# Softmax over 16384 rows: four of eight loads, and their stores, as four transfers of every fourth partition

## The chip, the core and the metric

The kernel runs on one core of one Trainium2 chip. The metric is the device time of one execution in microseconds (us); lower is better. Times given are medians of several runs. An execution under the profiler gives the trace and its page; the page's span runs from the first to the last recorded instruction.

## The reference

```
def setup_inputs():
    batch, seq, dim = 16, 1024, 512
    return {"x": np.random.randn(batch, seq, dim).astype(np.float32)}

def reference(x):
    x_max = np.max(x, axis=-1, keepdims=True)
    exp_x = np.exp(x - x_max)
    return (exp_x / np.sum(exp_x, axis=-1, keepdims=True)).astype(np.float32)
```

It is a softmax over the last dimension: 16384 rows of 512 fp32 values, 33.55 MB read and 33.55 MB written.

## The kernel before

The 16384 rows are cut into 16 groups of 1024 rows; a group (2 MB) is 8 rows on each of the 128 partitions. Two groups make one load and one store of 4 MB, so there are eight loads, L0 to L7, and eight stores, S0 to S7; store k writes the rows that load k brought. In a load, partition p gets 16 neighbouring rows of x, which is one run of 32 KB in the memory, and the 128 partitions together one run of 4 MB (`in_dram`, where x is viewed as `"(p r) d -> p r d"`). A store is the same in the other direction.

In SBUF the groups lie in a ring of 12 places (`RING`), six loads. So L0 to L5 need no wait, and L6 and L7 take the places of L0 and L1 and have to wait until S0 and S1 have landed (`before`, `stored`).

All transfers are issued by SP, on one queue. The first six loads are issued at the head of the program, the very first one even ahead of the opening barrier (`AT_HEAD`, `loads_at_the_head`). A closing barrier of the head (`tc.close()`, line 179) follows the six; the other engines begin their work after it. After that SP goes through a list written by hand:

```
ORDER = """
S0 S1 L6 L7 S2 S3 S4 S5 S6 S7
"""
```

Before a store SP waits until both groups of it are scaled (`store_scaled`), before L6 and L7 until the store of the old rows has landed. At the end it waits for the stores that are still out (line 200). The queue works in the order of issue.

The compute on a group g has three steps. VectorE (DVE) takes the negated maximum of each row (`rowmax`, line 145; one instruction for one or two groups), once the load has landed. ScalarE (ACT) computes the exponential in place with the maximum as bias and the row sum as a second output (`exp`, line 134; 8 rows for each partition and group, one instruction for each, in a loop `exps` over the groups). Then DVE takes the reciprocal of the sums (line 159), and DVE or GpSimd (POOL) multiplies the group by it (line 161, `scale`). DVE's order is written out too:

```
SEQUENCE = """
M0 M1 M2 D0 M3 D1 MM4 P2 MM6 D3 P4 MM8 D5 P6 MM10 D7 P8 MM12 D9 P10 MM14 D11 P12 D13 D14
D15
"""
```

M and MM are maxima of one and two groups, D a scaling on DVE and P one on POOL. Each load has a semaphore of its own, `loaded`; the DMA engines add 16 to it when a transfer has landed.

Of the kernel before, what the change touches and what calls it, by code (L numbers as in the profile page):

```python
# [15 lines left out]
GROUP = 8  # L16
# [4 lines left out]
STORES = [2, 2, 2, 2, 2, 2, 2, 2]  # L21
GROUPS = sum(LOADS)
LOAD_AT = [sum(LOADS[:k]) for k in range(len(LOADS))]
STORE_AT = [sum(STORES[:k]) for k in range(len(STORES))]

ORDER = """
S0 S1 L6 L7 S2 S3 S4 S5 S6 S7
# [32 lines left out]
@with_exitstack  # L60
def kernel(
    ctx: ExitStack,
    tc: tile.TileContext,
    x: bass.AP,
    out: bass.AP,
):
    nc = tc.nc
    nc.at_finalize(loads_at_the_head)
    P = nc.NUM_PARTITIONS

    x_rows, out_rows = x.flatten_outer_dims(), out.flatten_outer_dims()
    d = x_rows.shape[1]
    assert x_rows.shape[0] == P * GROUPS * GROUP

    def sbuf(name, n):
        return ctx.enter_context(nc.sbuf_tensor(name, [P, n], F32))

    ring = sbuf("ring", RING * GROUP * d)

    stat = sbuf("stat", RING * GROUP)  # L80
    recip = sbuf("recip", RING * GROUP)

    def sem(name):
        return ctx.enter_context(nc.semaphore(name))

    maxima, summed, inverted = [sem(s) for s in ("maxima", "summed", "inverted")]
    loaded = [sem(f"loaded{k}") for k in range(len(LOADS))]
    scaled = [sem(f"scaled{k}") for k in range(len(STORES))]

    def load_of(g):  # L90
        return max(k for k in range(len(LOADS)) if LOAD_AT[k] <= g)

    def store_of(g):
        return max(k for k in range(len(STORES)) if STORE_AT[k] <= g)


    before = {
        k: store_of(LOAD_AT[k] + LOADS[k] - 1 - RING)
        for k in range(len(LOADS))
        if LOAD_AT[k] >= RING  # L100
    }

    awaited = sorted(set(before.values()))
    stored = {k: sem(f"stored{k}") for k in awaited}
    others = sem("others")

    def at(g):
        return g % RING

    def rows(g, groups=1):  # L110
        part = ring[:, at(g) * GROUP * d : (at(g) + groups) * GROUP * d]
        return part.rearrange("p (r d) -> p r d", d=d)

    def cols(t, g, groups=1):
        return t[:, at(g) * GROUP : (at(g) + groups) * GROUP]

    def in_dram(t, g, groups):
        k = load_of(g)
        assert load_of(g + groups - 1) == k
        part = t[P * GROUP * LOAD_AT[k] : P * GROUP * (LOAD_AT[k] + LOADS[k]), :]  # L120
        first = (g - LOAD_AT[k]) * GROUP
        part = part.rearrange("(p r) d -> p r d", p=P)
        return part[:, first : first + groups * GROUP, :]

    def load(k):
        g, n = LOAD_AT[k], LOADS[k]
        return nc.sync.dma_start(out=rows(g, n), in_=in_dram(x_rows, g, n))

    def store(k):
        g, n = STORE_AT[k], STORES[k]  # L130
        return nc.sync.dma_start(out=in_dram(out_rows, g, n), in_=rows(g, n))

    def exp(row, one):
        return nc.scalar.activation(  # L134
            out=row, in_=row, func=EXP, bias=one, scale=1.0, accum_out=one
        )

    def spread(t):
        return t.unsqueeze(2).to_broadcast([P, GROUP, d])


    def rowmax(g, groups):
        assert load_of(g) == load_of(g + groups - 1)
        nc.vector.wait_ge(loaded[load_of(g)], 16)  # L144
        nc.vector.reduce_max(  # L145
            out=cols(stat, g, groups), in_=rows(g, groups), axis=AX, negate=True
        ).then_inc(maxima, groups)

    def exps():
        with nc.Fori(0, GROUPS, 1, engines=(ACT,)) as g:  # L150
            nc.scalar.wait_ge(maxima, 1).then_inc(maxima, -1)  # L151
            row = nc.scalar.snap((g % RING) * GROUP)
            for r in range(GROUP):
                done = exp(ring[:, bass.ds((row + r) * d, d)], stat[:, bass.ds(row + r, 1)])
            done.then_inc(summed, 1)

    def scale(g, engine):
        nc.vector.wait_ge(summed, g + 1)
        nc.vector.reciprocal(out=cols(recip, g), in_=cols(stat, g)).then_inc(inverted, 1)  # L159
        engine.wait_ge(inverted, g + 1)  # L160
        engine.tensor_mul(  # L161
            out=rows(g), in0=rows(g), in1=spread(cols(recip, g))
        ).then_inc(scaled[store_of(g)], 1)

    def done_by(k):
        later = [a for a in awaited if a >= k]
        return stored[later[0]] if later else others

    def store_scaled(k):
        nc.sync.wait_ge(scaled[k], STORES[k])  # L170
        store(k).then_inc(done_by(k), 16)


    with tc.manual_schedule(engines={SP}):
        for k in range(min(before)):
            first = load(k).then_inc(loaded[k], 16)
            tc.info.no_tile_sem_insts.add(first.ins.name)
    tc.close()
    tc.compile()  # L179

    nc.scalar.preload_act_table(EXP)  # L181
    exps()
    for work in SEQUENCE.split():
        kind = work.rstrip("0123456789")
        g = int(work[len(kind) :])
        if kind in ("M", "MM"):
            rowmax(g, len(kind))
        else:
            scale(g, nc.vector if kind == "D" else nc.gpsimd)
    for transfer in ORDER.split():  # L190
        k = int(transfer[1:])
        if transfer[0] == "S":
            store_scaled(k)
        else:
            last = before[k]
            since = max([a for a in awaited if a < last], default=-1)
            nc.sync.wait_ge(stored[last], 16 * (last - since))
            load(k).then_inc(loaded[k], 16)
    nc.sync.wait_ge(others, 16 * (len(STORES) - 1 - max(awaited)))
    nc.sync.nop()  # L200


# [28 lines left out]
```

## Time and profile before

| | before |
|---|---|
| median of 3 runs | 160.0 us (159.95 to 160.03) |
| the profiled execution's own time | 160.08 us |
| its span | 158.8 us |
| DVE busy | 121.8 us (77%) |
| ACT busy | 92.2 us (58%) |
| POOL busy | 42.3 us (27%) |
| DMA queue | 67.11 MB in 2304 packets, 98.9% of 16 engines' span, 423 GB/s in the mean |

On the page the DMA line gives the mean busy share of the core's 16 DMA engines in tenths, in 40 slices of the span (9 is 90% or more). A packet is what one DMA engine moves in one piece: here a run of 32 KB, or a completion of 4 bytes, which adds to the semaphore. In the rows by stage the columns are: the stretch in us and its length, the busy time of DVE, ACT and POOL in it with the number of instructions, the clock of TensorE (which has no work here), the DMA engines' share and the GB/s they moved. "SPq" is the issuing of a transfer by SP; the transfer itself takes place later, on the DMA engines.

### The profile page before, as it was taken

The page shows a single profiled execution, that of the slowest core. Times are in us where ns is not written, and L with a number is a line of the kernel's source. Part 1 is how long each engine was busy: PE and PEld are TensorE (multiplying, and loading weights), DVE is VectorE, ACT ScalarE, POOL GpSimd, SP SyncE. Part 2 cuts the span into 40 slices and gives each one's busy share as a digit, 9 for nine tenths or more (in the row PEclk, how much of TensorE's full clock was granted, in tenths as well). Part 3 has the DMA queues.
Part 4 walks back from the last instruction along what each step waited for, and adds up shares of the span by engine and source line. Part 5 has one row for each costly group of instructions (what it writes and reads, how often), then busy time and mean ns, then how long its engine had stood idle before and what let it go on. Part 6 is the DMA issues. An engine that isn't in the chain of part 4 may idle for free.

```text
span 158.8 us, 572 instructions
## 1 busy us (share of the span) xinstructions
DVE 121.8 (77%) x36; ACT 92.2 (58%) x257; POOL 42.3 (27%) x10
## 2 busy tenths in 40 slices
DVE  0008979999999999999999499999999999700000
ACT  0300699969406999999988990899599300000000
POOL 0000000000007903930970790079049300000000
DMA  7999999999999999999999999999999999999996
GB/s 264 438 479 405 405 495 421 396 438 471 413 405 438 471 405 396 396 413 471 438 396 462 446 413 405 454 421 438 438 421 446 413 446 438 438 421 438 429 429 264
DMA packets 2304, 67.11 MB, mean 423 GB/s; under 512 B 256, under 2 KB 256, under 8 KB 256
## 3 DMA queue, kind: packets, MB, share of 16 engines
q1 hardware_dynamic: 2304, 67.11, 98.9%
HBM read 33.55 MB, written 33.55 MB: 423 GB/s over the span
## 4 chain that ended last, share of the span: by engine, by line
DMA 45%; DVE 39%; issue 2%; DVEq 0%
DMA ring<-in_x_dram 26%; DVE ring L161 22%; DMA out_dram<-ring 20%; DVE stat L145 16%; DVE recip L159 1%; DVEq L144 0%
## 5 line engine op out<-in xcount | busy, mean ns | idle before, releaser
L134 ACT ACTIVATE ring<-ring,stat x128 | 90.4, 707 | 28.1 <-ACTq L151 28.1
L145 DVE TENSOR_REDUCE stat<-ring 128x16 f32<-128x8192 f32 (+1 forms) x10 | 69.5, 6956 | 15.7 <-DMA ring<-in_x_dram 15.7
L161 POOL TENSOR_TENSOR ring<-ring,recip 128x4096 f32<-128x4096 f32 x6 | 42.1, 7016 | 81.8 <-DVE recip L159 81.8
L161 DVE TENSOR_TENSOR ring<-ring,recip 128x4096 f32<-128x4096 f32 x10 | 51.1, 5109 | 0.3
L134 ACT ACTIVATION_READ_ACCUMULATOR ring<-ring,stat x128 | 23.8, 186 | 0.0
L181 ACT ACT_TABLE_LOAD x1 | 1.3, 1283 | 4.0 <-PEq L179 4.0
L159 DVE RECIPROCAL recip<-stat 128x8 f32<-128x8 f32 x16 | 3.0, 190 | 0.0
L215 POOL MEMSET const-float32-0.0<- 128x1 f32 x1 | 0.1, 98 | 0.2 <-issue 0.2
L215 POOL MEMSET const-bfloat16-1.0<- 128x1 bf16 x1 | 0.1, 102 | 0.0
L215 POOL MEMSET const-uint8-127<- 128x1 uint8 x1 | 0.1, 102 | 0.0
L215 POOL MEMSET const-float32-1.0<- 128x1 f32 x1 | 0.1, 98 | 0.0
## 6 DMA issues: line engine op xcount, KB each, us to landing
ring<-in_x_dram SPq DMA_DIRECT2D x8, 4096.0 KB, 25.9
out_dram<-ring SPq DMA_DIRECT2D x8, 4096.0 KB, 24.0
```

The costliest lines, as they stand in the source:

```text
L134: return nc.scalar.activation(out=row, in_=row, func=EXP, bias=one, scale=1.0, accum_out=one)
L145: nc.vector.reduce_max(out=cols(stat, g, groups), in_=rows(g, groups), axis=AX, negate=True).then_inc(maxima, groups)
L159: nc.vector.reciprocal(out=cols(recip, g), in_=cols(stat, g)).then_inc(inverted, 1)
L161: engine.tensor_mul(out=rows(g), in0=rows(g), in1=spread(cols(recip, g))).then_inc(scaled[store_of(g)], 1)
L181: nc.scalar.preload_act_table(EXP)
L215: nc = _bacc.Bacc("TRN2", target_bir_lowering=False, num_devices=1)
```

## The change

A list `PIECES` gives for each load the number of transfers that it is made of: four for loads 0, 2, 5 and 7, one for the others. Where it is four, the load's 4 MB in the memory are cut into four pieces of 1 MB, each one run. Piece j goes to the partitions j, j + 4, j + 8 and so on, 32 of them, 16 rows (32 KB) to each. So other partitions than before hold the rows. The store of the same rows uses the same pieces. All are issued by SP, one after the other, where the one transfer was issued. They add to the same semaphore as the one transfer did, and the waits are for four times 16. The first load's first piece alone stands ahead of the opening barrier, since `AT_HEAD` still says one. The instructions of DVE, ACT and POOL are the same.

```
+PIECES = [4, 1, 4, 1, 1, 4, 1, 4]
...
-        part = part.rearrange("(p r) d -> p r d", p=P)
-        return part[:, first : first + groups * GROUP, :]
-
-    def load(k):
+        n = PIECES[k]
+        part = part.rearrange("(n q r) d -> n q r d", n=n, q=P // n)
+        return [part[j, :, first : first + groups * GROUP, :] for j in range(n)]
+
+
+    def load(k, done):
         g, n = LOAD_AT[k], LOADS[k]
-        return nc.sync.dma_start(out=rows(g, n), in_=in_dram(x_rows, g, n))
-
-    def store(k):
+        ones = [
+            nc.sync.dma_start(out=rows(g, n)[j :: PIECES[k]], in_=part).then_inc(done, 16)
+            for j, part in enumerate(in_dram(x_rows, g, n))
+        ]
+        return ones
+
+    def store(k, done):
         g, n = STORE_AT[k], STORES[k]
-        return nc.sync.dma_start(out=in_dram(out_rows, g, n), in_=rows(g, n))
+        by = PIECES[load_of(g)]
+        for j, part in enumerate(in_dram(out_rows, g, n)):
+            nc.sync.dma_start(out=part, in_=rows(g, n)[j::by]).then_inc(done, 16)
+
+    def store_count(first, last):
+        return 16 * sum(PIECES[load_of(STORE_AT[k])] for k in range(first, last))
...
-        nc.vector.wait_ge(loaded[load_of(g)], 16)
+        nc.vector.wait_ge(loaded[load_of(g)], 16 * PIECES[load_of(g)])
...
-        store(k).then_inc(done_by(k), 16)
+        store(k, done_by(k))
...
-            first = load(k).then_inc(loaded[k], 16)
-            tc.info.no_tile_sem_insts.add(first.ins.name)
+            for one in load(k, loaded[k]):
+                tc.info.no_tile_sem_insts.add(one.ins.name)
...
-            nc.sync.wait_ge(stored[last], 16 * (last - since))
-            load(k).then_inc(loaded[k], 16)
-    nc.sync.wait_ge(others, 16 * (len(STORES) - 1 - max(awaited)))
+            nc.sync.wait_ge(stored[last], store_count(since + 1, last + 1))
+            load(k, loaded[k])
+    nc.sync.wait_ge(others, store_count(max(awaited) + 1, len(STORES)))
```

## The prediction

> **What bounds the kernel now.** I read the page first, from its busy shares and its queue to its chain, then the rate stage by stage, then the joints between transfers in the trace's packet records.
>
> ```profile
> span 158.8 us, 572 instructions
> DVE 121.8 (77%) x36; ACT 92.2 (58%) x257; POOL 42.3 (27%) x10
> ...
> DMA  7999999999999999999999999999999999999996
> ...
> DMA packets 2304, 67.11 MB, mean 423 GB/s; under 512 B 256, under 2 KB 256, under 8 KB 256
> q1 hardware_dynamic: 2304, 67.11, 98.9%
> ```
>
> No compute engine is full, but the sixteen DMA engines are busy in every slice. Of the 2304 packets 256 are completions (16 transfers on 16 engines); the other 2048 are rows of 32 KB, 128 for each engine. 98.9% of 158.8 us over 128 rows is 1.227 us a row, and in the packet records 1.213 us is the usual one. 128 x 1.213 = 155.3 us, so only some 3.5 us of the span are anything but rows at their steady rate.
>
> The page's chain crosses DVE lines (39%), which could mislead: it follows the semaphores back, and the last store waits there for nothing but the queue. S7 is issued at 137.84, right after the last DVE multiply, while S6, issued at 128.69, ends near 148.1; S7's rows move from 148.1 to 158.27. So compute has 10 us in hand at the end. Earlier, L6 is issued at 71.08, when S1's rows are still moving until 79.8, and S2 at 81.46, when L6 and L7 have the queue until 99.6. The queue never runs dry, and the time is that of the DMA stream alone.
>
> The rates by stage show where the 3.5 us lie (the stages are cut where transfers begin; the last column is GB/s):
>
> ```profile
> 0.00:11.60 11.60, 0.00 (x0) 1.28 (x1) 0.20 (x4) 1.00 0.93 376
> 11.60:50.40 38.80, 37.03 (x11) 24.33 (x69) 1.68 (x1) 1.00 1.01 435
> 50.40:60.70 10.30, 10.27 (x3) 10.30 (x29) 5.34 (x1) 1.00 1.00 404
> 60.70:89.80 29.10, 27.57 (x10) 27.94 (x81) 15.41 (x3) 1.00 1.00 434
> 89.80:99.60 9.80, 8.87 (x3) 5.60 (x16) 5.64 (x1) 1.00 1.01 428
> 99.60:158.80 59.20, 38.07 (x12) 22.80 (x64) 14.03 (x2) 1.00 0.97 421
> ```
>
> 435 GB/s is the steady rate. L0 runs at 376: 11.6 x (1 - 376/435) = 1.57 us lost, 1.04 of it before the first packet, 0.53 in the slow first rows. L5, the load ahead of the first store, runs at 404: 10.3 x (1 - 404/435) = 0.73 us. L7, the load ahead of S2, runs at 428: 0.16 us. The rest is the tail: the engines' last rows end between 157.06 and 158.27, and the last landing is at 158.73. The packet records agree: L5's last row on each engine takes 1.79 us in the mean instead of 1.213, L7's 1.36, L0's first 1.92; at the other joints, loads after loads, stores after stores and L6 after S1, the rows keep their pace within 0.01 us in the mean. On the engine that I follow to the latest end, 158.27, these stretches are 0.62 (start), 0.96 (L5 to S0) and 0.41 us (L7 to S2).
>
> The profiled execution took 160.08 us, 1.28 more than its span; the median is 160.0. I make the sum against 160.08 and take the 0.08 off at the end.
>
> **The change part by part.** *Bytes and rows*: nothing is removed. Every row still has 32 KB in both memories, so there are still 2048 rows, 128 x 1.213 us for each engine if each transfer of 32 rows is spread over all sixteen, two rows each. No instruction of DVE, ACT or POOL changes in size or number.
>
> *Completions*: loads 0, 2, 5, 7 and stores 0, 2, 5, 7 are four transfers each: 24 more, so 24 more completions on every engine. A completion takes 9 ns in the packet records, and at the fifteen joints between transfers the next row starts 2 to 3 ns after the last one's end, against 3 to 4 ns before its end inside a transfer: 6 ns a joint. 24 x 6 ns = +0.14 us; bounds, below 0 no (work is added), above 0.22 (24 x 9) by this row.
>
> *Issues*: SP issues 15 transfers at the head instead of 6. Six took 3.17 us (0.33 to 0.52 each, barrier included); with up to 0.5 for each piece the head ends near 7.5. Behind it wait the closing barrier and ACT's table load, at 3.97 now:
>
> ```profile
> 0.00 3.17 SPq L127 DMA_DIRECT2D ring<-in_x_dram  x6
> ...
> 3.97 1.28 ACT L181 ACT_TABLE_LOAD   x1 [3.97 <-PEq L179]
> 12.37 4.42 DVE L145 TENSOR_REDUCE stat<-ring 128x8 f32<-128x4096 f32 x1 [12.37 <-DMA ring<-in_x_dram]
> ```
>
> DVE's first work waits for L0 until 12.37, so this costs nothing; 4 us of cover are left, and beyond that the compute reserve of 8 to 10 us. The first piece alone stands ahead of the opening barrier, the second is issued at about 0.8; a piece lasts two rows, 2.4 us and more, so the queue stays fed. Later pieces add up to 1.4 us to an issue: S0 (ready at 39.96, moves at 60.7), L7 (81.07 for 89.8), S2 (moves at 99.6) and S7 (137.84 for 148.1) have 8 us and more. Behind S0's pieces SP waits for S1 until 61.79 anyway, behind L7's stands S2, which is early. No wait of the page becomes later.
>
> *Waits*: DVE waits for four pieces in place of one load; they end together with the load's last row. Nothing.
>
> *The first transfer*: the sixteen engines start their first row between 1.04 and 1.69 us, mean 1.22, while the 128 rows of L0 are being issued. A transfer of 32 rows should reach the last engine sooner: at most -0.18 us in the mean and -0.65 on the last; but the pieces behind it come later, which by the barrier row (0.43 to 0.79) could cost +0.3. I take -0.1.
>
> *The two turns from loads to stores*: L5, S0, L7 and S2 are all pieced, so both sides of both turns change shape, the sixteen engines working in 1 MB of x or out instead of 4 MB. Steady rows are at 1.213 either way, so a gain can come only here. Bounds: -1.37 us (0.96 + 0.41, all of it, on the last engine), and above 0 the same again, if twice as much is lost. No row shows a turn between pieces; the nearest row is the spread among the turns themselves, 0.58 us in the mean at one and 0.15 at the other, which says that the loss isn't fixed but hangs on how the engines' rows lie to each other. I take -0.5, somewhat over a third of the last engine's loss.
>
> Sum: 160.08 + 0.14 - 0.1 - 0.5 = 159.62; less 0.08, 159.5, and as the second turn alone may be all that is won, I put it at **159.6 us**.
>
> *Who moves the rows*: a transfer of 32 rows is not in the trace of before. [...] Bounds: 0, and +77.6 us (64 rows of each engine at twice 1.213, if two always meet). I take 0, the row of every steady transfer. [...]
>
> **The rivals.** *No change (160.0 to 160.1).* The turns cost what loads before stores cost, whatever the shape: +0.14 - 0.1 is left. For it: the 128 rows at 1.213 are fixed and hold 98% of the stream. Against: the two turns differ fourfold now.
>
> *Slower: two engines meet on one way, or pieces stretch at their joints.* Place: the 64 rows of each engine in pieces. It decides from 5 ns a row on (0.32 us), which gives 160.3. Were each of the 24 new joints stretched by L7's 0.15 us, it is +3.6, 163.6; by L5's 0.58, +13.9, 174; if rows always meet, 238. For it: nothing of before has moved 32 rows at a time, and L5 shows that a row can be stretched by half. Against: joints between transfers of the same kind lose nothing.
>
> *Slower: every completion holds up its engine until the write is confirmed.* The last row ends at 158.27, the last landing is at 158.73: 0.46 us x 24 = +11, 171 us. Against it: fifteen joints now at 6 ns each. [...]
>
> *Slower: SP is held at the head.* If fewer than 15 transfers may be outstanding, say eight, SP issues the last of L5 when seven have landed, near 26 us, and the barrier and all compute come some 14 us later than 12.37: 4 to 6 us more than the reserve, 165. Against: six of 4 MB were taken at once.
>
> **How the numbers follow.** Forecast, a smaller loss at the turns and the start: 0.42, its own range 159.0 to 159.75. No change: 0.25. Meeting or stretched rows: 0.28, of which 0.17 under 161.4 (up to 0.05 us a joint, 24 x 0.05 = 1.2). Held completions 0.03, held SP 0.02. What the measurement can tell from no change is about 0.2%, 0.3 us, so faster 0.42, same 0.25, slower 0.33. The range goes from 158.9 (0.03 below it) to 161.4 (0.11 + 0.03 + 0.02 above it).
>
> **What would show it.** Right: 128 rows an engine at 1.213, 10.3 us of L5 shortened by about half a microsecond, 640 completions, SP's head at 6 to 8 us, ACT's table load after it and DVE's first start still near 12.4. Wrong: a rate clearly under 435 in the stretches of L2, S5 or S7 (rows meet), L5 still at 404 (no change), DVE's first start late (SP held), or a new idle time of the DMA engines at every piece.

## The result and the profile after

The changed kernel takes 161.31 us (median of 4 runs, 160.88 to 162.48) beside 160.01 us of the kernel before (159.95 to 160.03). The ratio is 1.0093, with a 95% interval from 1.0069 to 1.0116: slower by 0.9%, where I had forecast 159.6. Run again later it took 160.85 us (160.71 to 161.82) beside 159.97, a ratio of 1.0074 (1.0052 to 1.0096). Not only the median is worse: its runs lie up to 1.6 us apart, those of before beside them within 0.1 us. (Of 67 later runs of before one took 161.22 us, all others 160.54 or less.)

The page of the changed kernel, profiled in an execution of 160.88 us, the shortest of the four:

```profile
span 159.6 us, 596 instructions
DVE 121.8 (76%) x36; ACT 92.2 (58%) x257; POOL 42.3 (27%) x10
...
DMA packets 2688, 67.11 MB, mean 421 GB/s; under 512 B 640, under 2 KB 640, under 8 KB 640
...
q1 hardware_dynamic: 2688, 67.11, 98.5%
```

The bytes and the compute are the same, and the completions are the 640 that were expected. The span is 0.8 us longer. Rates by stage, cut where transfers begin in this kernel (columns as before, GB/s last):

```profile
0.00:12.40 12.40, 0.00 (x0) 1.28 (x1) 0.20 (x4) 1.00 0.89 346
12.40:51.20 38.80, 36.48 (x11) 23.77 (x67) 1.13 (x1) 1.00 1.01 435
51.20:61.20 10.00, 9.97 (x3) 10.00 (x29) 5.89 (x1) 1.00 1.02 426
61.20:90.40 29.20, 28.42 (x10) 28.05 (x81) 14.67 (x3) 1.00 1.00 431
90.40:100.20 9.80, 8.75 (x2) 6.34 (x18) 6.39 (x1) 1.00 1.01 428
100.20:159.60 59.40, 38.19 (x13) 22.80 (x64) 14.03 (x2) 1.00 0.97 419
```

The stretch of L1 to L4 runs at the old 435 GB/s, although L2 is now in pieces: in the steady stream a piece costs nothing that a rate shows. L5 runs at 426 instead of 404, the gain that I had looked for. And the head has fallen to 346 GB/s over 12.4 us instead of 376 over 11.6. Added up from the packet records, as means over the sixteen engines: the first row starts 0.51 us later (1.73 for 1.22), the rows of the head lose 0.34 us more (1.08 for 0.74), the first turn loses 0.40 less (0.27 for 0.68), the second is the same, and the joints and idle times cost 0.22 more. That is +0.67 for the mean engine. The last engine ends 0.79 us behind the mean instead of 0.53, and the last landing follows its row 0.14 us sooner: +0.80 us.

SP's part at the head, in the timeline:

```profile
0.00 9.88 SPq L132 DMA_DIRECT2D ring<-in_x_dram  x15
...
10.92 1.28 ACT L194 ACT_TABLE_LOAD   x1 [10.92 <-PEq L192]
13.72 4.42 DVE L158 TENSOR_REDUCE stat<-ring 128x8 f32<-128x4096 f32 x1 [13.72 <-DMA ring<-in_x_dram]
```

The 15 issues take 9.88 us instead of the 7.5 that I had reckoned, and ACT's table load moves from 3.97 to 10.92. It is still hidden: DVE waits for L0 until 13.72. What is late is the load itself.

### The profile page after: what moved, and what is told of

Read it like the earlier page. It is cut to its first block, busy times and chain, and to the rows that moved or that the text cites. A ratio compares the mean times of both kernels' runs of the same rounds, so it can differ in the third digit from the quotient of the medians.

```text
span 159.6 us, 596 instructions
## 1 busy us (share of the span) xinstructions
DVE 121.8 (76%) x36; ACT 92.2 (58%) x257; POOL 42.3 (27%) x10
## 3 DMA queue, kind: packets, MB, share of 16 engines
q1 hardware_dynamic: 2688, 67.11, 98.5%
## 4 chain that ended last, share of the span: by engine, by line
DMA 43%; DVE 39%; issue 2%; SPq 2%; DVEq 0%
DMA ring<-in_x_dram 25%; DVE ring L174 22%; DMA out_dram<-ring 18%; DVE stat L158 16%; SPq L141 1%; SPq L132 1%; DVE recip L172 1%; DVEq L157 0%
```

## Three theories and the experiments

Theory A: the loss is made at the head, by load 0's pieces. Theory B: it is spread over the joints, each costing the same. Theory C: it is the layout, 1 MB in one run in the memory instead of rows from all over 4 MB. For the experiments the changed kernel's one list became three, so that the number of transfers of a load, that of a store and the layout can be set apart:

```
+LOAD_IN = [...]; STORE_IN = [...]; RUNS = [...]
...
+        if n == by:    # n = RUNS[k]; by = LOAD_IN[k] or STORE_IN[k]
+            part = part.rearrange("(n q r) d -> n q r d", n=n, q=P // n)
+            return [part[j, :, first : first + groups * GROUP, :] for j in range(n)]
+        part = part.rearrange("(p r) d -> p r d", p=P)
+        return [part[j::by, first : first + groups * GROUP, :] for j in range(by)]
```

With RUNS 1 a partition keeps the rows that it had before; a piece is still every fourth partition.

| kernel | median us (range) | ratio to before (95%) | first row, us | longest third or fourth row, us | first turn, us |
|---|---|---|---|---|---|
| before | 159.88 to 159.97 (159.59 to 161.22) | | 1.04 | 1.23 | 0.68 |
| changed, first profile | 161.31 (160.88 to 162.48) | 1.0069 to 1.0116 | 1.40 | 2.48 | 0.27 |
| changed, again | 160.85 (160.71 to 161.82) | 1.0052 to 1.0096 | 1.37 | 1.38 | 0.93 |
| load 0 whole | 160.16 (159.85 to 160.55) | 1.0003 to 1.0027 | 1.02 | 1.24 | 0.77 |
| only load 0 and store 0 in pieces | 160.72 (160.40 to 162.74) | 1.0023 to 1.0078 | 1.37 | 1.75 | 0.35 |
| changed, four ahead of the barrier | 160.66 (160.58 to 160.82) | 1.0028 to 1.0057 | 1.36 | 1.32 | 0.94 |
| changed, old layout | 160.62 (160.54 to 160.72) | 1.0024 to 1.0053 | 1.36 | 1.23 | 0.76 |
| only load 0 and store 0, old layout | 160.84 (160.36 to 162.74) | 1.0045 to 1.0113 | 1.36 | 1.85 | 0.87 |
| changed, load 0 and store 0 old layout | 161.77 (160.65 to 162.09) | 1.0062 to 1.0123 | 1.35 | 2.48 | 0.71 |
| stores 0 and 2 in pieces | 160.05 (159.87 to 160.25) | 0.9996 to 1.0016 | 1.02 | 1.22 | 0.63 |
| load 0 in four by columns | 159.90 (159.65 to 160.14) | 0.9985 to 1.0007 | 1.03 | (8 KB rows) | 0.81 |
| load 0 in four of neighbours | 169.52 (169.38 to 169.73) | 1.0581 to 1.0614 | 1.03 | 2.57 | 0.04 |
| load 0 and store 0, old layout, four ahead | 160.34 (160.22 to 161.15) | 1.0018 to 1.0042 | 1.39 | 1.24 | 0.86 |
| before, eight engines held back | 160.94 (160.85 to 160.95) | 1.0046 to 1.0072 | 1.00 | 1.23 | 0.05 |

The last three columns are from the packet records of the one execution whose trace each kernel left: the earliest row of any engine, the longest third or fourth row (a piece is two rows on an engine, so these are the second piece's), and what the rows around the turn from L5 to S0 take beyond 1.213 us, mean over the engines. The line "before" gathers the three later sets of runs. The last four kernels ran on another chip than the nine from "changed, again" to "stores 0 and 2 in pieces": before took 159.88 us beside the four, 159.92 and 159.97 beside the nine. Each ratio is to the runs of before beside it. Where an engine waits without a row, the column of the longest row doesn't count it.

**Load 0 whole again.**

```
+LOAD_IN = STORE_IN = RUNS = [1, 1, 4, 1, 1, 4, 1, 4]
```

> Load 0 and store 0 are whole again; loads and stores 2, 5 and 7 stay in four pieces (18 more transfers than before, not 24). Theory A (the loss is made at the head, where the first, small transfer starts late and 15 issues of 0.6 us each follow): most of the loss goes, 159.7 to 160.1 us, and the first load lands near 12.4 us as before. Theory B (each new joint costs the same, 1.3 us over 24 = 0.054 us): 161.0 us. Theory C (runs of 1 MB instead of 4 MB in the memory slow the rows while the stream is new): 160.0 to 160.3, like A.

160.16 us, near A's end and far from B's 161.0. The first row is back at 1.02. The 18 joints that are left cost 0.24 us in the medians (0.05 to 0.43 by the interval), 0.013 us each; B is out.

**Only load 0 and store 0 in pieces.**

```
+LOAD_IN = STORE_IN = RUNS = [4, 1, 1, 1, 1, 1, 1, 1]
```

> Only load 0 and store 0 are four pieces, all the others whole. A: 160.0 + 0.85 (late start 0.51, slow first rows 0.34) + 6 x 0.009 = 160.9 us if the pieces of load 0 alone make it; about half of that if the 15 issues do, since only nine stand at the head here. B: 160.3 us. C: 160.9.

160.72 us, near A's 160.9: a quarter of the pieces brings most of the loss, and the spread too. Its trace shows one thing that the table's column of longest rows hides. Five engines, done with their first piece between 4.48 and 4.63 us, begin the third row only between 5.28 and 5.65: each stood idle for 0.65 us or more, one of them for 1.0 or more. The rate of the stage shows it:

```profile
2.40:5.00 2.60, 0.00 (x0) 0.00 (x0) 0.00 (x0) 1.00 0.80 340
5.00:7.50 2.50, 0.00 (x0) 0.39 (x1) 0.00 (x0) 1.00 0.93 341
```

**All four pieces of load 0 ahead of the opening barrier.**

```
-AT_HEAD = {mybir.EngineType.SP: 1}
+AT_HEAD = {mybir.EngineType.SP: 4}
```

> The changed kernel with all four pieces of load 0 ahead of the opening barrier instead of one. A, in the form that the barrier between the first and the second piece starves the queue: the rows of piece two are at 1.213 us and the time falls by 0.3 us or more, to 161.0 or less. A, in the form that the issues themselves cost: 161.3, since they are the same. B and C: 161.3.

160.66 us within 0.24 us. That is 0.65 under the 161.31 that the theories started from, but only 0.19 under the changed kernel's 160.85 when it was run again on this chip (below), and the two intervals overlap: how much the median falls isn't settled, the spread is what differs. No third row over 1.32, where the changed kernel's first profile has 2.48; the first row is as late as before the edit (1.36). So there seem to be two losses at the head: a fixed one of a third of a microsecond, and one that comes and goes.

**The pieces, but the old layout.**

```
+LOAD_IN = STORE_IN = [4, 1, 4, 1, 1, 4, 1, 4]
+RUNS = [1, 1, 1, 1, 1, 1, 1, 1]
```

> The pieces stay (every fourth partition, 24 more transfers), but each partition holds the rows that it held before: a piece is 32 runs of 32 KB, one in every 128 KB of the 4 MB, not one run of 1 MB. A and B: 161.3 us, since the number of issues and joints is the same. C: 160.0 to 160.4, and the rows of the first 10 us are as short as before.

160.62 us within 0.18 us. Neither 161.3 nor 160.0 to 160.4; the first row is late here too, but no row is slow. It looked as if the layout made the slow rows, which the next runs were to settle.

**The changed kernel again.**

> The changed kernel itself once more, beside the kernels below and for its spread. If the slow rows of the first ten microseconds (0.34 us in its one profile beyond those of before) differ from execution to execution: 160.8 to 162.5 us with a median near 161.2, against 0.2 us of spread where the pieces keep the old rows. If its wide spread was the other chip's: near 160.7, with 0.3 us of spread.

160.85 us, but up to 161.82: the wide spread is its own. This profile has no row as in the first one. The same stretches of the head in both, first the first profile:

```profile
2.40:5.00 2.60, 0.00 (x0) 0.00 (x0) 0.00 (x0) 1.00 1.05 403
5.00:7.50 2.50, 0.00 (x0) 0.00 (x0) 0.00 (x0) 1.00 0.76 288
7.50:10.00 2.50, 0.00 (x0) 0.00 (x0) 0.00 (x0) 1.00 1.00 419
```

and the second one, of the same code:

```profile
2.40:5.00 2.60, 0.00 (x0) 0.00 (x0) 0.00 (x0) 1.00 0.95 403
5.00:7.50 2.50, 0.00 (x0) 0.00 (x0) 0.00 (x0) 1.00 1.00 419
7.50:10.00 2.50, 0.00 (x0) 0.00 (x0) 0.00 (x0) 1.00 0.98 419
```

288 GB/s where the second piece's rows move, against 419: the loss that comes and goes is there. And the turn from L5 to S0, which was 426 GB/s in the first profile, is back at the rate of before in the second:

```profile
11.90:50.70 38.80, 37.10 (x11) 24.58 (x70) 1.75 (x1) 1.00 1.01 434
50.70:61.40 10.70, 10.66 (x3) 10.70 (x31) 5.27 (x1) 1.00 1.03 407
```

So the gain at the turn, which the first comparison of the two kernels shows, is no property of the change.

**Only load 0 and store 0, old layout.**

```
+LOAD_IN = STORE_IN = [4, 1, 1, 1, 1, 1, 1, 1]
+RUNS = [1, 1, 1, 1, 1, 1, 1, 1]
```

> Only load 0 and store 0 in four pieces, each partition with the rows it held before. Theory A1 (a transfer of 32 rows at the head starts the stream 0.3 us later, whatever its layout, and a joint costs 6 to 9 ns): 160.0 + 0.3 + 0.05 = 160.3 us, narrow. Theory C1 (beyond that, load 0's runs of 1 MB make rows three to six slow): this one lacks them, and is 0.3 to 0.4 us under the 160.7 of the same pieces with runs of 1 MB. Rival: the slow rows come with the pieces in any layout: 160.7 and wide.

160.84 us and up to 162.74, as wide as with runs of 1 MB, and a third row of 1.85. C1 is wrong.

**The changed kernel, load 0 and store 0 in the old layout.**

```
+RUNS = [1, 1, 4, 1, 1, 4, 1, 4]
```

> The changed kernel, but load 0 and store 0 alone keep the old rows on each partition; loads and stores 2, 5 and 7 have their runs of 1 MB. C1 (the slow rows come from load 0's layout): 160.6 us and narrow, like the pieces that all keep the old rows. Rival (the layout of the later pieces counts too): 161.0 or more.

161.77 us, up to 162.09: C1 wrong once more. The layout is out as a cause. This is the one profile, among the kernels that begin with every fourth partition, of an execution over 161 us (161.76), and it shows best how the loss works; the runs above that, up to 162.74, have no trace. In it one engine, done with its first piece, stands idle from 4.67 to 5.49 us, and another takes 2.48 us for its third row. Two engines then begin their sixth row at 9.47 and 9.60, the next latest at 8.59; at the end two engines have their last row done at 159.83 and 160.05, the next latest at 159.15, the mean at 158.55. The last rows of the two late engines began at 158.62 and 158.84, when the other engines but one had already ended theirs (between 157.97 and 158.54): nobody takes over what one engine has lost, and the kernel ends with the last engine.

**Only the stores at the turns in pieces.**

```
+LOAD_IN = RUNS = [1, 1, 1, 1, 1, 1, 1, 1]
+STORE_IN = [4, 1, 4, 1, 1, 1, 1, 1]
```

> All loads whole and all rows where they were; only stores 0 and 2, the first after a load each time, are four pieces (6 joints more). Theory of the prediction (the shape of the transfers at the turns sets what they cost): the first turn at some 0.35 us in the mean instead of 0.68, and 159.6 to 159.8 us. Rival T (the first turn costs the less the farther the engines have drifted apart by then, whatever the shape): drift as before, so 0.65 to 0.9 us at the turn and 160.0 to 160.1.

160.05 us, no change that can be told, and the first turn at 0.63. (Here the stores alone are in pieces. With L5 in pieces too, the turn was 0.71 to 0.94 us in five profiles of the table and 0.27 in one.) Its stage runs at the rate of before, to the number:

```profile
50.40:60.70 10.30, 10.27 (x3) 10.30 (x30) 5.22 (x1) 1.00 1.00 404
```

**Load 0 in four by columns**, each transfer of all 128 partitions; edit to the kernel before:

```
+            if k == 0:
+                to, of = rows(0, 2), in_dram(x_rows, 0, 2)
+                ones = [nc.sync.dma_start(out=to[:, 4 * j : 4 * j + 4], in_=of[:, 4 * j : 4 * j + 4]) for j in range(4)]
```

> The kernel before, with load 0 alone in four transfers, but of all 128 partitions and 8 KB on each (four of a partition's sixteen rows); store 0 whole. Theory H (a transfer of few rows takes SP and the stream longer to begin: 0.58 us of issue and a first row at 1.37 us in every kernel that begins with 32 rows, 0.39 and 1.04 with 128): issue near 0.39, first row near 1.04, 160.0 to 160.2 us. Rival (any cut of load 0 with one piece ahead of the barrier does it): first row near 1.35, 160.4 us or more, and wide.

159.90 us, no change, within 0.5 us; first row at 1.03. Cutting load 0 in four with one part ahead of the barrier is harmless as such.

**Load 0 in four of 32 neighbouring partitions**, the same edit with `to[32 * j : 32 * j + 32]` and `of[32 * j : 32 * j + 32]`.

> The kernel before, with load 0 alone in four transfers of 32 neighbouring partitions each, store 0 whole. Theory H: issue near 0.58 us and first row near 1.37, as with every fourth partition. Rival (the step of four partitions is what takes longer to issue): 0.39 and 1.04. [...]

169.52 us. The issue of its first transfer, in the timeline of SP:

```profile
0.00 0.39 SPq L178 DMA_DIRECT2D ring<-in_x_dram  x1
```

and the same issue in the changed kernel:

```profile
0.00 0.58 SPq L132 DMA_DIRECT2D ring<-in_x_dram  x1
```

Both are transfers of 32 rows of 32 KB from one run of 1 MB. The first issue of the kernel before, of all 128 rows:

```profile
0.00 0.38 SPq L127 DMA_DIRECT2D ring<-in_x_dram  x1
```

The first row comes at 1.03 us here, at 1.37 to 1.40 in the changed kernel and at 1.04 in the kernel before. So theory H is wrong: it is not a transfer of few rows that is slow to begin, but one with a step of four partitions. The rows then move at half the rate:

```profile
0.00:21.30 21.30, 0.00 (x0) 1.28 (x1) 0.20 (x4) 1.00 0.98 208
21.30:60.10 38.80, 36.58 (x11) 23.88 (x67) 1.23 (x1) 1.00 1.00 426
60.10:70.40 10.30, 10.27 (x3) 10.30 (x31) 5.79 (x1) 1.00 1.01 433
```

208 GB/s and rows of 2.55 us for 1.213, about twice as long; what holds them up isn't shown. The engines stay busy (0.98), as they are when all is well (1.01 at 435 GB/s over L1 to L4 of before); the rate tells the difference, not the share.

**Load 0 and store 0 in pieces, old layout, four ahead of the barrier.**

```
-AT_HEAD = {mybir.EngineType.SP: 1}
+AT_HEAD = {mybir.EngineType.SP: 4}
```

> Load 0 and store 0 in four pieces with the old rows, all four pieces of load 0 ahead of the opening barrier (with one ahead: 160.84 us, 160.36 to 162.74). Theory B1 (the wide spread and the slow third rows come from the barrier between the first piece and the second, which leaves an engine without a row to go on with): 160.3 to 160.5, with less than 0.4 us of spread, no third row over 1.4 us. Rival (four pieces of 32 rows at the head do it, barrier or not): 160.7 or more and wide.

160.34 us, eleven of twelve runs within 0.28 us and one at 161.15; with one ahead it was 160.84 and 2.4 us wide. No third row over 1.24. B1 fits, with that one run as a reminder that the head isn't wholly steady. The run with one ahead was on the other chip; but there, too, the changed kernel with four ahead stayed within 0.24 us. Over all kernels that begin with every fourth partition, 15 of 44 runs took over 161 us with one piece ahead of the barrier, one of 18 with four ahead, and one of 71 of the kernel before.

**Eight engines held back**; edit to the kernel before, behind load 0:

```
+                some = x_rows[0:128, :].rearrange("(p r) d -> p r d", p=8)[:, 0:6, :]
+                held = nc.sync.dma_start(out=spare[0:8].rearrange("p (r d) -> p r d", d=d), in_=some)
```

> The kernel before, and behind load 0 one transfer more of eight rows of 12 KB into a spare place, which nothing reads: it holds eight of the sixteen engines back by some 0.45 us. Theory T (the first turn from loads to stores costs the less the farther apart the engines stand): the drift among the engines at 45 us rises from 0.17 to about 0.28 us, the first turn falls from 0.68 us in the mean to 0.45 or less, and the time stays within 0.3 us of 160.0. Rival (the turn's cost is a matter of chance or of shapes): the turn stays at 0.63 to 0.94, and the time rises by 0.25 us or more.

The turn is gone, 0.05 us, and L5's stage runs at 430 GB/s:

```profile
11.60:50.60 39.00, 35.56 (x11) 22.86 (x65) 0.21 (x1) 1.00 1.00 421
50.60:61.20 10.60, 10.57 (x3) 10.60 (x31) 6.80 (x1) 1.00 1.00 430
```

So the turn did as T said, but the time, 160.94, did not, because the small transfer slowed L1's first row on the other engines as well (2.3 us on each of the eight that had no part in it): 421 GB/s over L1 to L4. As for T, the drift at the 45th row (standard deviation over the engines) and the turn go together in part of the kernels: 0.42 and 0.05 here, 0.26 and 0.27, 0.34 and 0.35, 0.12 and 0.93. They don't in others: 0.37 and 0.71 (load 0 and store 0 in the old layout), 0.17 and 0.04 (neighbours) beside 0.17 and 0.68 (before). T as I put it is wrong.

## Why the prediction was wrong

*What bounds the kernel, and the steady rows*: right. The DMA stream alone sets the time (98.5% of 16 engines' span in the changed kernel), and every piece in the steady stream moves at 1.213 us a row. Who moves the rows, the term that I took at 0 between 0 and 77.6 us, was rightly judged for every fourth partition: the pieces' rows took 1.213 us in the median and 1.214 in the mean (L2 in the changed kernel). For 32 neighbours 0 would have been wrong: rows of 2.55 us, +9.6 us for one load. What makes the difference isn't shown.

*Completions*: the estimate of 6 ns a joint, 0.14 us in all, was about right. From before to the old layout's pieces the time between rows grew by 0.18 us over 24 joints, of which 0.04 are two idle times at the turn: 6 to 7 ns each. The rival that every completion holds up its engine is refuted: by its own price 18 more would be 8 us (0.46 each), and they cost 0.24.

*Issues*: the cost was right (nothing), the size too small. Most of the 15 issues take 0.58 us or more, up to 0.87, where I had reckoned with 0.5 at most, and the second piece is issued at 1.22 us, not at about 0.8. It stays hidden: ACT's table load, now at 10.92, ends at 12.20, and DVE starts at 13.72.

*The first transfer*: **this is the step that failed.** I took -0.1 us, as 32 rows should be issued sooner than 128, with +0.3 for the barrier as the far end. Measured, the engines start 0.51 us later in the mean (1.73 for 1.22), beyond that end, and the earliest row comes 0.31 to 0.36 us later in each of the eight profiles that begin with every fourth partition, and 0.01 to 0.04 sooner in the five new ones that don't. What failed is the premise: a transfer with a step of four partitions is not issued sooner, its first issue takes 0.58 us where that of 128 rows takes 0.38. Beyond that the second piece's rows can be late or slow, in the profiles by over 1 us on one engine (a row of 2.48 us, a wait of 1.0 or more); runs went up to 162.74 us. I had bounded the mean of the engines; the end is set by the slowest one. And I wrote that a piece lasts 2.4 us "so the queue stays fed": an engine without a next row from 4.67 to 5.49 us, while SP had issued that piece by 1.72 us, shows that issued is not the same as at hand.

*The turns*: **the second step that failed**, a size that was none. I took -0.5 us out of the difference between the two turns of one execution. The first profile's -0.40 looks like a hit but is luck: the turn's cost differs from execution to execution of one kernel, 0.27 and 0.93 us in the changed one, and its mean over the six profiles with pieces on both sides, 0.73, is no lower than the 0.68 of before.

*The rivals*: the outcome is on the slower side, to which I gave 0.33, and in no rival's place: not at the joints, not by rows that meet (1.213 us a row in the pieces), not by SP being held. Within the range's 158.9 to 161.4 the median of 161.31 lies near the upper end, but the side was wrong.

What the runs show: the steady part of the loss is the late first row (0.3 us) and the joints (0.2). In the profiled executions of the old layout and of before, 160.60 and 160.08 us, that is all of it; the medians of that set, 160.62 and 159.92, are 0.2 farther apart, which isn't assigned. The rest, and the spread, goes with the barrier between the first piece and the second: with the four pieces ahead of the barrier the spread falls from 2.4 to 0.3 us, bar one run, and with a first transfer of neighbouring or of all partitions, one ahead of the barrier, it stays at 0.5 us or less. Not every handful of runs shows it: the six of the old layout, with one piece ahead, were narrow too. What stays open: why the second piece's rows are sometimes not at hand. In the three profiles where an engine idled there, SP's issue at 4.2 us took 0.87 to 1.03 us, in two profiles of the same 15 issues without it 0.63; this hints at the issues, not at the memory, but which waits for which isn't shown. Open too is what sets the cost of the first turn from loads to stores. No kernel tried here beats the one before.

## What to carry to other kernels

When a stream of transfers already fills the DMA engines, count what is left outside the steady rows, and ask first what a change does to the start: a piece that is cheap in the stream (here 6 to 7 ns) can cost a third of a microsecond as the first transfer (here one to every fourth partition, with the first row at 1.35 to 1.40 us for 1.00 to 1.04), and an engine that falls behind early can be the last at the end (here one that began its sixth row about a microsecond late ended at 160.05 us, with the mean at 158.55). A stall that one profile shows may be chance; look at it in a second execution of the same kernel before pricing its removal. And watch the rate beside the busy share: with 32 neighbouring partitions the engines were 98% busy at 208 GB/s.

## What was not expected of the hardware

- The program's first transfer takes 0.58 us to issue when it goes to every fourth partition and 0.38 to 0.39 when it goes to 32 or 128 neighbouring ones, and its first row comes 0.3 us later (1.35 to 1.40 for 1.00 to 1.04 us). Later issues don't divide so cleanly: whole loads behind pieces took 0.58 to 0.60 us too.
- Transfers to 32 neighbouring partitions move at 208 GB/s with the engines at 98% busy, in rows of 2.55 us; to every fourth partition the rows take 1.213 us, as in whole loads.
- A DMA engine can stand idle for 0.82 us, in another profile for 1.0 us or more, before a row whose transfer SP had issued more than 3 us before the row began.
- The turn from the loads to the first store cost 0.27 and 0.93 us an engine in two executions of one kernel, and anything between 0.04 and 0.94 over all these profiles, with the loads and stores in the same order.
